# Scale and shift after a turn: one pass from PSUM on ScalarE and VectorE in place of two passes on VectorE and GpSimd

## The chip, the cores and the metric

The kernel runs on one core of a Trainium2 chip. The metric is the device time of one execution in microseconds (us), lower is better; it is given as the median of several executions. The engines are called by the profile's names: PE (TensorE matmul), PEld (TensorE weight load), DVE (VectorE), ACT (ScalarE), POOL (GpSimd) and SP (SyncE, here the queue that issues the transfers). A line number such as L352 is a line of the kernel before.

## The reference, cut to what matters

The model is a two-layer transformer over 512 latent tokens and 256 context tokens of width 1024. Each sub-layer is preceded by an RMS norm with a scale and a shift per channel; the feed-forward of layer 0 is followed by the norm that feeds layer 1's mixer, and that norm is what the change touches.

```python
def rms_norm(x, g):
    xf = x.astype(jnp.float32)
    y = xf * lax.rsqrt(jnp.mean(xf * xf, -1, keepdims=True) + NORM_EPS)
    return (y * g.astype(jnp.float32)).astype(x.dtype)

def modulate(h, shift, scale):
    return h * (1.0 + scale) + shift

for i in range(DEPTH):
    ...
    u = modulate(rms_norm(h, g_pre_mix[i]), sh_m, sc_m)
    uc = modulate(rms_norm(hc, g_pre_mix[i]), csh_m, csc_m)
    ...
    f = swiglu(modulate(rms_norm(h, g_pre_ffn[i]), sh_f, sc_f), w_ffn_gate[i], w_ffn_up[i], w_ffn_down[i])
    h = h + gt_f * rms_norm(f, g_post_ffn[i])
    ...
```

## The kernel before

Products are made of three float32r matmuls each: every operand is split into a high part (`hi`, a rounding copy on ACT, L181) and a low part (`lo`, a subtraction on DVE or POOL, L182), and the three cross products hi·hi, hi·lo and lo·hi are added up in PSUM. So ACT and DVE do a pass over every weight and every activation before PE can use it.

The tokens lie in six tiles of 128: tiles 0 to 3 are the latent tokens, 4 and 5 the context. The down product of layer 0's feed-forward (`dn`, L1696 to L1698) is made in three passes: the first 512 channels for all six tiles, then the second 512 channels for tiles 0 to 3, then the second 512 channels for tiles 4 and 5. In each pass a loop over 22 blocks of the hidden dimension loads weights (`raw_wd`), splits them (`hi_wd`, `lo_wd`), splits the block of hidden values (`gh` on ACT, `gl` on POOL in layer 0), and issues three matmuls for each tile.

When a tile of the second or third pass is complete, its rows are normed, gated and added to the residual `h` (`hbuf`, L1732 to L1739), and the generator `post_ffn0` hands it to `norm_T` (L341). `norm_T` takes the sum of squares (L337), the power -0.5 on POOL (L221, L228), scales the rows into `hn` (L345), and then, for each half of 512 channels, lets PE turn four blocks of 128x128 into one PSUM bank (`ptp`, L350), multiplies by the channel's scale from PSUM into `nt` (L352, DVE), adds the channel's shift in place (L353, POOL), and splits `nt` into `u1h` and `u1l`, the input of layer 1 (L181, L182). After the turn a channel is a partition, so scale and shift are one column (`a_col`, `s_col`) for each block of 128. `nt` has two buffers, `ptp` two banks. For latent tiles each half is split in two instructions of 128x256, because the tokens are also reordered; for context tiles in one of 128x512.

So the norm of tiles 0 to 3 runs while PE does the third pass of the down product (tiles 4 and 5), and the norm of tiles 4 and 5 while PE does the first product of layer 1 (`gq`, L523 to L525), which needs all four latent tiles. After it come four products for the neighbourhood attention's queries (`naqk`), then `gkv` and `nav`, which need the context tiles too. Beside them the modulation vectors of later norms are summed on DVE (`macc`, L254) from weights that SP fetches (`mraw`); their buffers lie in memory that the down product has used before.

The order of instructions on each engine is not the order of the program: the launch builds the kernel with a planner that keeps a simulated timeline and sorts the instructions of each engine by priority and by the times it expects. Each engine then runs its own list in order, so an instruction that waits holds everything behind it on that engine. SP issues its transfers in order too.

```python
with tile.TileContext(nc, schedule_with_timeline_sim=True) as tc:
    emit(tc, A)
...
ffn(0, U0, True, 6, close_u0, opened0, mods0, lambda: GGs['f0'], open_u1, post_ffn0)
...
tok_proj(A['wgq'], 512, range(4), lambda t, ps: head_norm(gqt[:, t, :], ps, 8, gqn, t, 1.0), uh, ul, "gq")
```

Of the kernel before, what the change touches and what calls it, by code (L numbers as in the profile page):

```python
# [154 lines left out]
AF = mybir.ActivationFunctionType  # L155
ALU = mybir.AluOpType
# [7 lines left out]
def emit(tc, A):  # L164
    nc = tc.nc
    V, S, G, T = nc.vector, nc.scalar, nc.gpsimd, nc.tensor
# [8 lines left out]
    def bc(ap, n):  # L175

        return ap.unsqueeze(len(ap.shape)).to_broadcast(list(ap.shape) + [n])

    def split(hi, lo, src, lo_eng=None):

        S.activation(hi, src, AF.Copy)  # L181
        (lo_eng or V).tensor_tensor(lo, src, hi.bitcast(F32), ALU.subtract)  # L182
# [151 lines left out]
    def rstd_of(src, junk):  # L334
        ss = sm.tile([128, 1], F32, tag="ss", name="ss")
        r = sm.tile([128, 1], F32, tag="rr", name="rr")
        S.activation(junk, src, AF.Square, scale=1.0 / 32.0, accum_out=ss)  # L337
        rsqrt_(r, ss, EPS)
        return r

    def norm_T(src, a_col, s_col, pst, hi_out, lo_out):  # L341

        hn = tmpp.tile([128, 1024], F32, tag="hn", name="hn", bufs=2)
        r = rstd_of(src, hn)
        S.activation(hn, src, AF.Copy, scale=r)  # L345
        yield
        for hf in range(2):
            ps = pst()
            for k in range(4):
                T.transpose(ps[:, k * 128:(k + 1) * 128], hn[:, (hf * 4 + k) * 128:(hf * 4 + k + 1) * 128], ident)  # L350
            t = tmpp.tile([128, 4, 128], F32, tag="nt", name="nt", bufs=2)
            V.tensor_tensor(t, ps.rearrange("p (k t) -> p k t", k=4), bc(a_col[:, hf * 4:hf * 4 + 4], 128), ALU.mult)  # L352
            G.tensor_tensor(t, t, bc(s_col[:, hf * 4:hf * 4 + 4], 128), ALU.add)  # L353
            for (h, l, sv) in zip(hi_out(hf), lo_out(hf), split_view(t, len(hi_out(hf)))):
                split(h, l, sv)

    class Lagged:

# [31 lines left out]
    def split_view(t, n):  # L390
        if n == 1:
            return [t]
        v = t.rearrange("p k (r b c) -> p k r b c", r=2, b=8)
        return [v[:, :, i] for i in range(2)]
# [36 lines left out]
    def ptp(name="ptp"):  # L431
        return bank("v", name)
# [181 lines left out]
    for d in range(2):  # L614
        rhs = gv[:, :, d * 8:(d + 1) * 8]
        ps = ptp("cum")
# [5 lines left out]
        ps = ptp("rest")  # L622
# [7 lines left out]
    for p in range(2):  # L630
        ps = ptp("tot")
# [1205 lines left out]
    def post_ffn0(t):  # L1837
        v = 0 if t < 4 else 1
        yield from norm_T(h[:, t, :], acol[v][:, 2, :], scol[v][:, 2, :], ptp, u_views(u1['h'], t), u_views(u1['l'], t))
# [470 lines left out]
```

## Time and profile before

| what | value |
|---|---|
| median of 3 runs | 1999.85 us (1995.31 to 2003.21) |
| the profiled execution | 1996.12 us |
| its span, first to last instruction | 1994.0 us |
| PE busy | 1830.4 us (92%) |
| DVE busy | 1436.1 us (72%) |
| ACT busy | 966.6 us (48%) |
| POOL busy | 928.0 us (47%) |
| mean granted TensorE clock | 0.956 |

The span is what the profile's rows cover; the execution's time is 2.1 us more. Busy shares are means over the whole span; the stretch that the change touches lies between 1229 and 1300 us and is read by itself below. A granted clock of 1.00 is TensorE's full level (2.4 GHz), 0.50 the half level (1.2 GHz).

### The profile page before, as it was taken

The numbers are of one execution on the slowest core, as the hardware profiler recorded it, in microseconds if no ns is written. First come the engines' busy times: TensorE is split into PE (matmuls) and PEld (weight loads), VectorE is DVE, ScalarE is ACT, GpSimd is POOL, SyncE is SP. The second block draws the span as 40 slices with busy tenths as digits, with TensorE's granted clock in tenths as the row PEclk, the third lists the DMA queues.
The fourth block names the chain that finished last, engine by engine and source line by source line (L and its number), as shares of the span: only waits on it lengthen the run. The fifth ranks groups of instructions, "written<-read, shape, count | busy, mean of one in ns | idle before, by whom it ended". The sixth has DMA issues, their size and how long they took to land.

```text
span 1994.0 us, 33781 instructions
## 1 busy us (share of the span) xinstructions
PE 1830.4 (92%) x12760; PEld 1504.2 (75%) x12760; DVE 1436.1 (72%) x2040; ACT 966.6 (48%) x1816; POOL 928.0 (47%) x828
## 2 busy tenths in 40 slices
PE   6989978989898979999999998889989959999998
PEld 3877855656566869999997776677655659999886
DVE  3686757677876696666656886887566589999654
ACT  4433457666874553333333345533455445445443
POOL 2387454344533376556547665653256142333101
PEclk7999978888999989999999999999999979999999
DMA  8255694665724613222227543586634212333221
GB/s 305 84 153 149 203 296 129 182 188 155 243 80 141 244 64 106 80 75 75 64 75 258 161 153 101 172 280 207 184 106 121 85 64 85 106 107 96 85 95 64
DMA packets 125751, 280.20 MB, mean 141 GB/s; under 512 B 12882, under 2 KB 43498, under 8 KB 125588
## 3 DMA queue, kind: packets, MB, share of 16 engines
q1 hardware_dynamic: 125588, 278.03, 44.0%
q8 instruction: 101, 1.65, 0.3%
q14 instruction: 62, 0.51, 0.1%
HBM read 226.15 MB, written 46.07 MB: 137 GB/s over the span
## 4 chain that ended last, share of the span: by engine, by line
PE 53%; DVE 9%; issue 4%; DMA 4%; POOL 3%; ACT 3%; SPq 0%; POOLq 0%; DVEq 0%; ACTq 0%
PE st L198 9%; PE st L199 9%; PE st L197 9%; PE dn L1696 4%; PE dn L1697 4%; PE dn L1698 4%; PE po L188 2%; DVE macc L254 2%; DMA mraw<-in_wmb_dram 2%; PE y L1410 1%; PE y L1411 1%; PE y L1412 1%; PE st L1958 1%; DVE ub L182 1%; PE st L1959 1%
## 5 line engine op out<-in xcount | busy, mean ns | idle before, releaser
L197 PE MATMUL st<-ub,hi_gu 128*128 128x384 f32 (+1 forms) x1232 | 385.8, 313 | 22.1 <-ACT ub L181 22.1
L198 PE MATMUL st<-ub,hi_gu 128*128 128x384 f32 (+1 forms) x1232 | 385.6, 313 | 1.1 <-DVE ub L182 1.0
L199 PE MATMUL st<-ub,lo_gu 128*128 128x384 f32 (+1 forms) x1232 | 384.3, 312 | 0.9 <-POOL lo_gu L182 0.9
L197 PEld LDWEIGHTS st<-ub,hi_gu 128*128 128x128 f32 x1232 | 233.9, 190 | 23.0 <-ACT ub L181 23.0
L199 PEld LDWEIGHTS st<-ub,lo_gu 128*128 128x128 f32 x1232 | 234.6, 190 | 1.6 <-POOL lo_gu L182 1.2
L198 PEld LDWEIGHTS st<-ub,hi_gu 128*128 128x128 f32 x1232 | 233.5, 190 | 2.0 <-DVE ub L182 2.0
L181 ACT ACTIVATE hi_gu<-s 128x512 fp32r<-128x512 f32 x176 | 111.1, 631 | 175.1 <-PE st L198 164.4
L1696 PE MATMUL dn<-hi_wd,gh 128*128 128x512 f32 x440 | 175.2, 398 | 2.2 <-ACT gh L181 2.2
L1697 PE MATMUL dn<-lo_wd,gh 128*128 128x512 f32 x440 | 175.0, 398 | 1.8 <-DVE lo_wd L182 1.8
L1698 PE MATMUL dn<-hi_wd,gl 128*128 128x512 f32 x440 | 165.3, 402 | 5.2 <-POOL gl L182 5.2
L182 DVE TENSOR_TENSOR lo_gu<-raw_gu,hi_gu 128x512 fp32r<-128x512 f32 x132 | 129.9, 998 | 42.8 <-ACT hi_gu L181 42.8
L182 DVE TENSOR_TENSOR lo_gu<-s,hi_gu 128x512 fp32r<-128x512 f32 x154 | 128.2, 833 | 45.1 <-ACT hi_gu L181 45.1
L254 DVE SCALAR_TENSOR_TENSOR macc<-mraw,cs,macc 128x1024 f32<-128x1024 f32 x80 | 125.5, 1592 | 22.8 <-DMA mraw<-in_wmb_dram 16.3
L181 ACT ACTIVATE hi_gu<-raw_gu 128x512 fp32r<-128x512 f32 x132 | 82.0, 629 | 98.8 <-PE st L198 91.9
L182 DVE TENSOR_TENSOR lo_wd<-raw_wd,hi_wd 128x512 fp32r<-128x512 f32 x110 | 96.8, 885 | 44.4 <-ACT hi_wd L181 44.3
L1606 POOL TENSOR_TENSOR s<-raw_gu 128x512 f32<-128x512 f32 x44 | 74.4, 1692 | 84.3 <-issue 70.7
L904 ACT ACTIVATE P<-st 128x512 f32<-128x512 f32 x128 | 73.0, 596 | 65.5 <-PE st L199 28.5
L1698 PEld LDWEIGHTS dn<-hi_wd,gl 128*128 128x128 f32 x440 | 82.3, 189 | 28.6 <-POOL gl L182 7.9
L1696 PEld LDWEIGHTS dn<-hi_wd,gh 128*128 128x128 f32 x440 | 83.0, 189 | 24.3 <-ACT gh L181 3.1
L181 ACT ACTIVATE gh<-g 128x512 fp32r<-128x512 f32 x76 | 47.5, 631 | 110.9 <-PE dn L1697 101.8
L1697 PEld LDWEIGHTS dn<-lo_wd,gh 128*128 128x128 f32 x440 | 83.0, 189 | 23.4 <-DVE lo_wd L182 2.7
L1662 POOL TENSOR_TENSOR g<-g,up 128x512 f32<-128x512 f32 x38 | 55.7, 1465 | 86.5 <-DVE up L1611 55.8
(545 smaller groups left out, 4794.7 us busy)
## 6 DMA issues: line engine op xcount, KB each, us to landing
mraw<-in_wmb_dram SPq DMA_DIRECT2D x56, 512.0 KB
raw_wd<-in_wd_dram SPq DMA_DIRECT2D x55, 512.0 KB
raw_gu<-in_wg_dram SPq DMA_DIRECT2D x44, 512.0 KB
raw_gu<-in_wu_dram SPq DMA_DIRECT2D x44, 512.0 KB
cu<-in_wmb_dram SPq DMA_DIRECT2D x24, 512.0 KB
raw_m<-in_wmb_dram SPq DMA_DIRECT2D x16, 512.0 KB
raw_qkv<-in_wqkv_dram SPq DMA_DIRECT2D x12, 512.0 KB
raw_tok<-qk_d SPq DMA_DIRECT2D x12, 512.0 KB
```

The lines of the kernel that those rows point to most:

```text
L181: S.activation(hi, src, AF.Copy)
L182: (lo_eng or V).tensor_tensor(lo, src, hi.bitcast(F32), ALU.subtract)
L197: T.matmul(out, wh, xh, start=start, stop=False)
L198: T.matmul(out, wh, xl, start=False, stop=False)
L199: T.matmul(out, wl, xh, start=False, stop=stop)
L254: V.scalar_tensor_tensor(a, raw, cs[:, self.k, v:v + 1], a, ALU.mult, ALU.add)
L904: S.activation(P[:, :n], ps[:, :n], AF.Exp)
L1606: G.tensor_tensor(s3, a11, a21, ALU.subtract)
L1662: G.tensor_tensor(g, g, u, ALU.mult)
L1696: T.matmul(ps, gh[:, tsl], wh, start=start, stop=False)
L1697: T.matmul(ps, gh[:, tsl], wl, start=False, stop=False)
L1698: T.matmul(ps, gl_[:, tsl], wh, start=False, stop=stop)
```

## The change

For each half of each tile the one multiply (DVE, 128x512) and the one add (POOL, 128x512) are replaced by four instructions of 128x128 that multiply and add in one pass from PSUM, with scale and shift as one value per partition: on ACT for the first half, on DVE for the second. Six tiles have two halves each, so 12 instructions of DVE and 12 of POOL go, and 24 of ACT and 24 of DVE come.

```diff
             t = tmpp.tile([128, 4, 128], F32, tag="nt", name="nt", bufs=2)
-            V.tensor_tensor(t, ps.rearrange("p (k t) -> p k t", k=4), bc(a_col[:, hf * 4:hf * 4 + 4], 128), ALU.mult)
-            G.tensor_tensor(t, t, bc(s_col[:, hf * 4:hf * 4 + 4], 128), ALU.add)
+            scaled(t, ps, a_col, s_col, hf)
             for (h, l, sv) in zip(hi_out(hf), lo_out(hf), split_view(t, len(hi_out(hf)))):
                 split(h, l, sv)
+
+    def scaled(x, ps, a_col, s_col, hf):
+
+        for k in range(4):
+            a, b = [c[:, hf * 4 + k:hf * 4 + k + 1] for c in (a_col, s_col)]
+            if hf == 0:
+                S.activation(x[:, k, :], ps[:, k * 128:(k + 1) * 128], AF.Identity, scale=a, bias=b)
+            else:
+                V.tensor_scalar(x[:, k, :], ps[:, k * 128:(k + 1) * 128], a, b, ALU.mult, ALU.add)
```

## Rows read from the trace of the kernel before

**Rows 1.** By stretch: length, busy PE, PEld, DVE, ACT, POOL (counts), PEclk, DMA share, GB/s

```profile
1236.25:1272.40 36.15, 28.82 (x133) 21.63 (x131) 36.15 (x46) 26.10 (x57) 31.72 (x35) 1.00 0.38 119
1272.40:1300.00 27.60, 26.94 (x127) 22.45 (x128) 21.69 (x31) 15.59 (x26) 12.29 (x16) 1.00 0.67 209
1320.00:1340.00 20.00, 15.26 (x103) 14.85 (x103) 17.30 (x23) 3.36 (x7) 10.43 (x11) 0.83 0.88 294
```

**Rows 2.** Groups by line and shape, 1236.2 to 1272.4 us: busy, mean ns | idle before

```profile
L182 DVE TENSOR_TENSOR u1l<-nt,u1h 128x256 fp32r<-128x256 f32 x13 | 11.0, 881 | 0.0
L1698 PE MATMUL dn<-hi_wd,gl 128*128 128x512 f32 x32 | 10.9, 420 | 5.2 <-POOL gl L182 5.2
L353 POOL TENSOR_TENSOR nt<-nt,scol 128x512 f32<-128x512 f32 x8 | 10.5, 1307 | 3.9 <-DVE nt L352 3.5 <-PE dn L1698 0.5
L352 DVE TENSOR_TENSOR nt<-ptp,acol 128x512 f32<-128x512 f32 x8 | 5.3, 677 | 0.0
L181 ACT ACTIVATE u1h<-nt 128x256 fp32r<-128x256 f32 x14 | 5.0, 405 | 4.5 <-POOL nt L353 4.5
```

**Rows 3.** Timeline of PE: start, length, instruction [idle before, releaser]

```profile
1249.17 0.73 PE L1698 MATMUL dn<-hi_wd,gl 128*128 128x512 f32 x2 [0.89 <-POOL gl L182]
1260.90 0.73 PE L1698 MATMUL dn<-hi_wd,gl 128*128 128x512 f32 x2 [1.76 <-POOL gl L182]
1269.61 0.50 PE L523 MATMUL gq<-hi_gq,u1h 128*128 128x512 f32 x1 [1.50 <-ACT u1h L181]
1273.06 1.21 PE L525 MATMUL gq<-hi_gq,u1l 128*128 128x512 f32 x4 [1.34 <-DVE u1l L182]
```

**Rows 4.** Timeline of POOL: start, length, instruction

```profile
1240.21 1.23 POOL L353 TENSOR_TENSOR nt<-nt,scol 128x512 f32<-128x512 f32 x1
1241.40 1.18 POOL L182 TENSOR_TENSOR gl<-gm,gh 128x256 fp32r<-128x256 f32 x1
1246.83 0.83 POOL L221 TENSOR_SCALAR rr<-ssd 128x1 f32<-128x1 f32 x1
```

**Rows 5.** Groups by line and shape of ACT, whole span

```profile
L181 ACT ACTIVATE wo_h<-raw_o 128x1024 fp32r<-128x1024 f32 x8 | 8.3, 1055 | 6.8 <-DMA raw_o<-in_wo_dram 6.8
L345 ACT ACTIVATE hn<-hbuf,rr 128x1024 f32<-128x1024 f32 x6 | 6.9, 1148 | 4.2 <-POOL rr L228 4.2
L1664 ACT ACT_TABLE_LOAD x2 | 2.6, 1283 | 0.0
L1885 ACT ACTIVATE gkt<-gkv 128x128 f32<-128x128 f32 x6 | 1.8, 306 | 0.0
```

**Rows 6.** Timeline of ACT: start, length, instruction [idle before, releaser]

```profile
1241.64 0.71 ACT L181 ACTIVATE u1h<-nt 128x256 fp32r<-128x256 f32 x2
1278.30 1.15 ACT L345 ACTIVATE hn<-hbuf,rr 128x1024 f32<-128x1024 f32 x1 [0.61 <-POOL rr L228]
```

**Rows 7.** Groups by line and shape of DVE, whole span

```profile
L1609 DVE TENSOR_TENSOR p<-p,st 128x384 f32<-128x384 f32 x22 | 12.2, 553 | 18.4 <-PE st L199 18.4
L1609 DVE TENSOR_TENSOR p<-p,st 128x256 f32<-128x256 f32 x22 | 9.0, 409 | 0.4 <-PE st L199 0.2
L182 DVE TENSOR_TENSOR lo_wk<-raw_wk,hi_wk 128x128 fp32r<-128x128 f32 x4 | 1.3, 320 | 2.3 <-ACT hi_wk L181 2.3
```

**Rows 8.** Timeline of the DMA queue of SP

```profile
1279.48 0.33 SPq L1444 DMA_DIRECT2D hbuf<-in_gpost_dram  x1
1279.90 0.86 SPq L252 DMA_DIRECT2D mraw<-in_wmb_dram  x2
```

**Rows 9.** Timeline of PE, later

```profile
1322.12 0.38 PE L523 MATMUL gkv<-hi_gkv,u1h 128*128 128x256 f32 x1 [1.79 <-DVE xl L1923]
1329.77 0.58 PE L523 MATMUL gkv<-hi_gkv,u1h 128*128 128x256 f32 x1 [2.96 <-DVE xl L1923]
```

**Rows 10.** Busy time by stretch, the four us around the later waits

```profile
1326.00:1330.00 4.00, 1.04 (x8) 0.84 (x8) 3.11 (x3) 0.27 (x1) 3.70 (x4) 0.87 0.85 295
1330.00:1334.00 4.00, 4.00 (x20) 4.00 (x21) 3.04 (x4) 1.61 (x4) 1.21 (x2) 0.50 0.88 257
```

## Prediction, made blind

> **What bounds the kernel now.** The busy shares of the page make PE the bound over the whole span, but the change touches one stretch only, so I read that stretch by itself, in this order: the busy time by stretch, the groups of instructions inside it, the timelines of PE and POOL there, and then what SP and PE do behind it.
>
> In the stretch from the first turned tile to the last `u1h` of tile 3, 36.15 us, no engine has much room: DVE is busy all the time, POOL 31.7 us, PE 28.8 us, ACT 26.1 us [rows 1]. The reader should see that PE is not the bound here. Its matmuls wait 5.2 us in all, in six waits, all of them for `gl`, the low part that POOL makes [rows 2]. The timeline of POOL shows why: an add of the norm (L353, 1.23 us at 1240.21) stands in front of the `gl` that PE wants [rows 4], and in the order of POOL's list the same holds for five of the six waits, the longest (1.76 us) among them. The other one (0.89 us, at 1249.17) ends a `gl` behind the small powers of the norm, L221 and L228 [rows 3, 4]. After the down product PE waits twice more, 1.50 us for the first `u1h` and 1.34 us for the `u1l` of tile 3 [rows 3]: that is the latency of the norm itself. Together PE idles 5.2 + 1.5 + 1.34 = 8.0 us between 1236 and 1274 us. That is the pot, 0.4% of the execution.
>
> DVE is full partly because its subtractions are slow there: `u1l` of 128x256 takes 881 ns [rows 2], while a DVE instruction of the same shape with an input in PSUM takes 409 ns [rows 7].
>
> **The change, part by part.** *POOL loses 12 adds.* Eight lie in the stretch, 10.5 us at a mean of 1307 ns [rows 2]; POOL goes from 31.7 to about 21 us busy. The five waits behind an add are 5.2 - 0.9 = 4.3 us, and these I count as gained. The 0.9 us behind the powers stays.
>
> *DVE loses 12 multiplies and gets 24 narrow ones.* A multiply costs 677 ns [rows 2], all twelve 8.1 us. No row shows a DVE pass from PSUM of 128x128 with two column operands. From 128x384 to 128x256 the time falls from 553 to 409 ns, 144 ns for 128 columns [rows 7], so 128x128 would be about 265 ns; the high end is the 320 ns of a 128x128 subtraction with both inputs in SBUF [rows 7], the low end the 144 ns of its columns alone. 24 x 0.265 = 6.4 us (3.5 to 7.7), so DVE gains about 1.7 us over the six tiles (0.4 to 4.6), some 1.1 us of it in the four latent ones. With a third of POOL's work gone (10.5 of 31.7), I take a third of the delay off DVE's subtractions: 13 x (881 - 409) ns = 6.1 us on `u1l`, a third is 2 us. DVE is then no longer full at 36 us; about 33 us are left to do.
>
> *ACT gets 24 passes.* No row has an ACT pass with two column operands either. A copy of 128x128 from PSUM takes 306 ns [rows 5]. One column operand as scale costs 1148 - 1055 = 93 ns, the difference of two copies of the same size [rows 5]. The bias I bound between nothing and another 93 ns: 399 to 492 ns. Two passes in a row take 0.71 us where one takes 405 ns [rows 2, 6], so neighbours overlap by 0.10 us and a pass costs the queue 0.30 to 0.39 us. I take 0.38, since a second column should cost what the first does. The stretch gets 16 of them, 16 x 0.38 = 6.1 us (4.8 to 6.3), all six tiles 9.1 us (7.2 to 9.4). What hides them is ACT's idle time, 36.15 - 26.10 = 10.05 us [rows 1], if the stretch stays as long; queued behind them are the splits `gh` and `hi_wd`, for which PE would wait.
>
> The Trainium skill (ScalarE: Activation LUTs, What ACT_TABLE_LOAD costs) speaks against the first half on ScalarE in particular: it states 186 ns plus 0.833 ns a column, 93 ns for each column operand, and an overlap of 93 ns between neighbours. By that a pass is an estimated 479 ns, 386 ns in the queue, and 16 of them 6.2 us; that differs little from the 6.1 us above, and the trace's 93 ns for one operand agrees [rows 5].
>
> *The latency of a half* falls. Before, it is a DVE pass of 677 ns, a wait, a POOL pass of 1307 ns and then the split [rows 2]; after, four passes of ACT, about 1.6 us, with no other engine between them and the split `u1h` on ACT. The 1.50 us for `u1h` should go, the 1.34 us for `u1l` most likely too.
>
> **The sum.** At best PE gets 4.3 + 1.5 + 1.3 = 7.1 us. But ACT would then have 26.1 + 6.1 = 32.2 us of work in 36.15 - 7.1 = 29.05 us. If nothing of it can move, ACT sets the stretch at 32.2 us and the gain is 3.95 us. Some of it can move: the splits of the next product's weights sit in the stretch, and ACT is busy only 15.6 of the 27.6 us behind it [rows 1]. Between 4 and 7.1 us I take 5.
>
> Does the gain last? Behind the stretch the DMA queues are nearly full (share 0.88 from 1320 to 1340 us [rows 1]), so a later start of transfers could eat it. The transfer that opens this run, `hbuf` at 1279.48, goes out when `hn` of tile 4 is finished, 1278.30 + 1.15 [rows 6, 8], and SP holds the `mraw` loads behind it [rows 8]. Tile 4 comes out of the down product, so when PE ends that product 4 to 5 us earlier, the whole run of transfers moves with it. The change issues no transfer of its own. Tiles 4 and 5 are normed under `gq`, while PE is busy 26.9 of 27.6 us [rows 1]; their eight ACT and eight DVE passes cost nothing there, and 3 us of ACT if the cover were gone.
>
> The profiled execution took 1996.1 us, so the sum gives 1991. The median of the three runs lies 3.7 us higher, 1999.85; against it the same 5 us give 1995, my forecast.
>
> **The rivals.** *The gain is used up behind the stretch* (chance 0.22). The planner puts in order again everything from the changed tiles on, with its own durations; the sums of `macc` on DVE and the full DMA queues could take back 5 us. Time: 2000. For it: 0.88 DMA share. Against it: the run of transfers starts from tile 4, which comes earlier.
>
> *The next gap closes too* (0.18). At 1322 and 1329.8 us PE waits 1.79 and 2.96 us for DVE [rows 9], and after the second wait the granted clock is 0.50; in the eight us shown the missing clock is 4 x (0.13 + 0.50) = 2.5 us [rows 10]. A DVE list in another order could avoid both: 5 + 4.75 + 2.5 = 12 us, 1988. Nothing in the profile says that it will; the waits hang on `mraw` loads too.
>
> *ACT becomes the bound* (0.1, the other side). If the planner puts each block of four passes in front of the `gh` that PE wants next, all 24 are exposed: 24 x 0.38 = 9.1 us, and with one gap long enough for the half clock, 2.5 us more: +11.6 us, 2011. It decides from the point where ACT's work in the stretch exceeds the 36.15 us, that is with 10 us added; 6.1 are expected. For it: ACT is in order and PE reads `gh` within a few us. Against it: POOL's wait is the last to end today, not ACT's.
>
> *Another order makes one more gap* of the kind at 1322 to 1330 us, with no gain left: 4.75 + 2.5 = 7 us, 2007 (0.07).
>
> *The ACT function costs a table load.* The kernel before has no Identity; a load takes 1283 ns [rows 5], and two for each of six tiles would be 15 us. The Trainium skill (ScalarE: Activation LUTs, Table sets: the hidden batching unit) says that identity, like copy, is in every set; then there is none. I give it 0.02, at 2015.
>
> The forecast itself has what is left, 0.41, with 1991 to 1999 as its own range.
>
> **How the numbers follow.** This kernel can be told from no change at about 0.5%, 10 us. Faster by more than that needs the second rival, or the forecast with luck in the order: 0.18. Slower by more needs ACT as the bound, the table load, or half of the extra gap: 0.14. The rest, 0.68, is within 10 us. The range 1984 to 2008 reaches over the second rival to the extra gap and leaves out 0.17.
>
> **What would show it.** Right: no POOL add on nt; 24 ACT passes of 0.4 to 0.5 us and 24 DVE passes of about 0.27 us; PE's waits for `gl` down from 5.2 to about 1 us; the first `gq` matmul 4 to 6 us earlier than 1269.6; `hbuf` on SP equally earlier; `u1l` under 881 ns. Wrong: PE waiting for `gh` or `hi_wd` from ACT in the stretch, a table load there, or a `gq` that starts earlier while the end of the span does not move: then the order behind it, and not this edit's costs, made the time.

## The result, and the profile after

The changed kernel takes 1986.32 us (median of 4 executions, 1983.3 to 1988.37) beside 2001.53 us for the kernel before (4 executions); the ratio (changed over before, below 1 is faster) is 0.9945, with an interval of 0.9922 to 0.9969. The two medians alone lie further apart, 15.2 us or 0.9924, near the lower end of that interval. Two later comparisons of the same two kernels gave 0.9953 and 0.9966 (below). Of 2000 us these ratios are 11, 9.4 and 6.8 us. The forecast was 5 us and 1995.

The profiled execution after took 1986.34 us, its span is 1984.6 us; before these were 1996.12 and 1994.0 us. The page's busy times of the changed kernel:

```profile
PE 1828.9 (92%) x12760; PEld 1505.4 (76%) x12760; DVE 1429.4 (72%) x2052; ACT 972.6 (49%) x1840; POOL 917.0 (46%) x816
```

Here the change can be counted: DVE 24 - 12 = 12 instructions more, ACT 24 more, POOL 12 fewer. Nothing of this size says where the time went; the stretch does. Its groups by line and shape, 1230.1 to 1264.7 us, after (busy, mean ns | idle before; lines from 357 on are eight higher than before, so L1706 is L1698 of before):

```profile
L182 DVE TENSOR_TENSOR lo_wd<-raw_wd,hi_wd 128x512 fp32r<-128x512 f32 x14 | 11.0, 811 | 0.3 <-ACT hi_wd L181 0.3
L1706 PE MATMUL dn<-hi_wd,gl 128*128 128x512 f32 x32 | 10.6, 413 | 1.8 <-POOL gl L182 1.8
L182 DVE TENSOR_TENSOR u1l<-nt,u1h 128x256 fp32r<-128x256 f32 x16 | 6.9, 473 | 0.4 <-ACT u1h L181 0.4
L361 ACT ACTIVATE nt<-ptp,scol,acol 128x128 f32<-128x128 f32 x16 | 6.0, 460 | 0.0
L363 DVE TENSOR_SCALAR nt<-ptp,acol,scol 128x128 f32<-128x128 f32 x16 | 5.4, 400 | 0.1
```

Beside [rows 2]: PE's wait for `gl` is 1.8 us where it was 5.2; `u1l` takes 473 ns where it took 881; the two new passes take 460 ns on ACT and 400 ns on DVE. The weights' subtraction `lo_wd`, 811 ns after, is quicker too; in the kernel before, 1236.2 to 1272.4 us:

```profile
L182 DVE TENSOR_TENSOR lo_wd<-raw_wd,hi_wd 128x512 fp32r<-128x512 f32 x14 | 13.2, 954 | 0.0
```

These waits are left in PE's timeline of the changed kernel:

```profile
1241.57 0.73 PE L1706 MATMUL dn<-hi_wd,gl 128*128 128x512 f32 x2 [0.92 <-POOL gl L182]
1243.55 0.73 PE L1706 MATMUL dn<-hi_wd,gl 128*128 128x512 f32 x2 [0.23 <-POOL gl L182]
1249.53 0.73 PE L1706 MATMUL dn<-hi_wd,gl 128*128 128x512 f32 x2 [0.65 <-POOL gl L182]
1260.72 0.50 PE L531 MATMUL gq<-hi_gq,u1h 128*128 128x512 f32 x1 [2.28 <-ACT u1h L181]
...
1312.39 0.39 PE L531 MATMUL gkv<-hi_gkv,u1h 128*128 128x256 f32 x1 [1.01 <-DVE xl L1931]
1318.23 0.39 PE L531 MATMUL gkv<-hi_gkv,u1h 128*128 128x256 f32 x1 [2.83 <-DVE xl L1931]
```

Against [rows 3] three short waits for `gl` stand in place of six, and the wait for `u1l` (1.34) is gone. In POOL's list each of the three ends a `gl` directly behind a power (L228). But the wait for `u1h` has grown from 1.50 to 2.28 us. ACT's timeline of the changed kernel shows what it was doing ahead of that `u1h`:

```profile
1255.58 1.51 ACT L361 ACTIVATE nt<-ptp,scol,acol 128x128 f32<-128x128 f32 x4
1256.95 1.18 ACT L181 ACTIVATE hi_gq<-raw_gq 128x512 fp32r<-128x512 f32 x2
1258.24 0.60 ACT L1733 ACTIVATE junk<-dn 128x512 f32<-128x512 f32 x1
...
1258.83 0.71 ACT L181 ACTIVATE u1h<-nt 128x256 fp32r<-128x256 f32 x2
1259.44 0.62 ACT L181 ACTIVATE hi_gq<-raw_gq 128x512 fp32r<-128x512 f32 x1
1259.96 0.71 ACT L181 ACTIVATE u1h<-nt 128x256 fp32r<-128x256 f32 x2
```

The four passes of tile 3's first half end at 1257.09, but two `hi_gq` splits and a sum of squares stand before its `u1h` in ACT's list, and one more split before the `u1h` of the second half, which ends at 1260.67; PE starts at 1260.72. ACT idles 0.1 us there in all. By stretch, after, with the columns of [rows 1] (first turned tile to the first `gq`, on to the first `gkv`, on to the last `nav`):

```profile
1230.10:1260.70 30.60, 26.50 (x125) 19.93 (x123) 29.87 (x56) 30.36 (x74) 22.97 (x28) 1.00 0.44 137
1260.70:1309.70 49.00, 48.90 (x212) 39.36 (x213) 40.81 (x57) 23.18 (x44) 20.06 (x21) 0.97 0.77 247
1309.70:1366.10 56.40, 52.56 (x297) 45.97 (x296) 42.92 (x51) 15.94 (x38) 30.89 (x28) 0.97 0.75 244
```

In the first row ACT is busy 30.36 and DVE 29.87 of 30.60 us: POOL has become free and two other engines are full. The third stretch in the kernel before, same view:

```profile
1318.60:1377.50 58.90, 53.82 (x297) 47.18 (x296) 46.31 (x55) 16.24 (x38) 33.55 (x31) 0.94 0.74 242
```

It was 2.5 us longer, with as many matmuls (297). In this pair of profiles that is the granted clock, 0.94 before and 0.97 after (58.9 x 0.06 = 3.5 us against 56.4 x 0.03 = 1.7), and the two waits for `xl`, 1.79 and 2.96 us before [rows 9], 1.01 and 2.83 after. But other profiles of the same kernels show something else. In two more of the kernel before (e1 and e11, below) the stretch is longer still, and its clock is 0.97 as well; the waits for `xl` add up to 4.4 to 4.8 us in three profiles before and to 3.8 to 4.7 in three after. What e1 and e11 have and no profile of the changed kernel does is a wait at a `nav` matmul, in e1:

```profile
1343.94 0.50 PE L523 MATMUL nav<-hi_nav,u1h 128*128 128x512 f32 x1 [3.17 <-ACT gvt L1886]
```

In e11 it is 3.38 us, in the first profile 0.34. ACT owes that `gvt`, and in e1 it stands behind another instruction in ACT's list, a sum of squares of `gq` (`hsq`) that waits for POOL:

```profile
1343.09 0.63 ACT L1874 ACTIVATE hsq<-gqt 128x512 f32<-128x512 f32 x1 [4.22 <-POOL gqt L387]
1343.63 0.26 ACT L1886 ACTIVATE gvt<-gkv 128x128 f32<-128x128 f32 x1
```

In ACT's list of the changed kernel this `hsq` stands three weight splits ahead of the first copies of `gkv`, and the wait is not there.

**A warning about two single profiles.** The two spans differ by 9.4 us, but the changed execution was already 6.2 us ahead at its first turned tile (1230.1 against 1236.3), before the norm comes into play, and each engine's list up to there is the same in both programs. So I compare stretches by their distance from the first turned matmul (L350), over three profiles of each kernel: before, e1 and e11 are the old one, after, e2 and e10 the new one. The columns are the start of the first matmul of `gq`, the first of `gkv`, the last of `nav`, and the end of the span, in us, each rounded for itself.

| kernel | first turn at | to `gq` | to `gkv` | to last `nav` | `gkv` to `nav` | to the end |
|---|---|---|---|---|---|---|
| before | 1236.3 | 33.3 | 82.4 | 141.2 | 58.9 | 757.7 |
| e1_same | 1233.3 | 33.4 | 83.1 | 143.2 | 60.2 | 762.8 |
| e11_same | 1241.7 | 33.4 | 83.6 | 144.0 | 60.5 | 764.0 |
| after | 1230.1 | 30.6 | 79.7 | 136.0 | 56.4 | 754.5 |
| e2_again | 1232.4 | 30.7 | 79.6 | 136.3 | 56.8 | 755.1 |
| e10_again | 1233.2 | 30.7 | 79.6 | 136.7 | 57.2 | 755.6 |

By the means the gain is 2.7 us up to `gq`, 0.7 us from `gq` to `gkv`, 3.1 us from `gkv` to the last `nav`, 6.5 us together, and 6.4 us at the end (761.5 against 755.1): what is won by the last `nav` is kept. The start of the first turn scatters over 8.4 us in the unchanged kernel alone, so I don't count the 6.2 us of lead. That it is chance is not shown: all three changed profiles have their first turn earlier than all three of the kernel before, by 5.2 us in the means, and more profiles would have to say whether a part of it belongs to the program.

### The profile page after: what moved, and what is told of

Read it like the earlier page. It is cut to its first block, busy times and chain, and to the rows that moved or that the text cites. A ratio compares the mean times of both kernels' runs of the same rounds, so it can differ in the third digit from the quotient of the medians.

```text
span 1984.6 us, 33787 instructions
## 1 busy us (share of the span) xinstructions
PE 1828.9 (92%) x12760; PEld 1505.4 (76%) x12760; DVE 1429.4 (72%) x2052; ACT 972.6 (49%) x1840; POOL 917.0 (46%) x816
## 4 chain that ended last, share of the span: by engine, by line
PE 63%; DVE 8%; ACT 5%; issue 3%; DMA 3%; POOL 2%; SPq 0%; POOLq 0%; ACTq 0%; DVEq 0%
PE st L197 10%; PE st L198 10%; PE st L199 10%; PE dn L1704 4%; PE dn L1705 4%; PE dn L1706 4%; PE po L188 3%; DVE macc L254 2%; PE y L1418 1%; PE y L1419 1%; PE y L1420 1%; PE st L1966 1%; PE st L1967 1%; PE rm L269 1%; PE naqk L197 1%
## 5 line engine op out<-in xcount | busy, mean ns | idle before, releaser
L1706 PE MATMUL dn<-hi_wd,gl 128*128 128x512 f32 x440 | 165.5, 403 | 1.8 <-POOL gl L182 1.8
L182 DVE TENSOR_TENSOR lo_gu<-raw_gu,hi_gu 128x512 fp32r<-128x512 f32 x132 | 130.2, 999 | 43.2 <-ACT hi_gu L181 43.1
L1706 PEld LDWEIGHTS dn<-hi_wd,gl 128*128 128x128 f32 x440 | 82.7, 190 | 25.3 <-POOL gl L182 4.4
```

The source lines that it names most:

```text
L1706: T.matmul(ps, gl_[:, tsl], wh, start=False, stop=stop)
```

## The experiments

The theory on trial is that of the prediction: POOL's adds stood before `gl`, their going is the gain, and it is kept as far as the engine that takes the work has room. Its rivals: the gain is DVE's own (narrow passes in place of wide ones), or it comes from the order that the planner makes behind the norm, or from chance. The expectations call the theory A and the rival of each run B or C. Every edit also lets the planner sort the lists anew, so an experiment rarely changes one thing alone.

**The kernels repeated.** e1_same is the kernel before, e2_again the changed kernel.

> The kernel before, unchanged: it says how far two builds of one program lie apart. My theory: about 6 of the 9.4 us between the two profiled spans arose ahead of the change's first instruction, where the order is the same, and are chance between executions; so the ratio here is 1.000 within 0.003, and the first turned tile of this profile (1236.3 us in the one shown) may lie anywhere between 1229 and 1238 us. Rival: the lead ahead of the change belongs to the changed program; then this profile has its first turned tile at 1236 us again, within 1.5 us.

> The changed kernel once more. My theory: only what happens from the first turned tile on is the change's, 3 to 6 us, ratio 0.997 to 0.9985; the first turned tile lies between 1229 and 1238 us as it falls out. Rival (the lead is the program's): ratio 0.9945 again, first turned tile at 1230 us again within 1.5 us.

Measured: e1_same 0.9984 (0.9971 to 0.9997), e2_again 0.9953 (0.9936 to 0.9970). The unchanged kernel can come out 0.16% beside itself, so a ratio's last 0.2% says little; the changed kernel lies outside that. Its ratio is below the 0.997 that I expected of the change alone, and its first turn, at 1232.4 us, is not where the rival had it: neither reading came out whole.

**One half at a time.** e3_act_half changes the first half only (ACT), e4_dve_half the second only (DVE):

```diff
-            scaled(t, ps, a_col, s_col, hf)
+            if hf == 0:            # e4: hf == 1
+                scaled(t, ps, a_col, s_col, hf)
+            else:
+                V.tensor_tensor(t, ps.rearrange("p (k t) -> p k t", k=4), bc(a_col[...], 128), ALU.mult)
+                G.tensor_tensor(t, t, bc(s_col[...], 128), ALU.add)
```

> Only the first half of each tile is changed (four passes of ACT from PSUM); the second half keeps the multiply on DVE and the add on POOL. My theory (POOL's adds stand in front of gl): half of the adds go, so PE's waits for gl fall from 5.2 to about 3 us, and the wait for u1h before the first gq matmul goes as in the full change; the norm's stretch gains 2 to 3.5 us, ratio 0.998 to 0.999. Rival (the narrow passes on DVE and its fewer, faster subtractions make the gain): no gain here, ratio 1.000.

> Only the second half of each tile is changed (four passes of DVE from PSUM); the first half keeps DVE and POOL. My theory: half of the adds go, waits for gl fall to about 3 us, but the first half's way through DVE and POOL stays, and with it the 1.5 us wait for u1h: gain 1.5 to 3 us, ratio 0.9985 to 0.9995. Rival (DVE's relief makes the gain): most of the full change's gain is here, 4 us or more after the first turned tile.

Measured: e3 0.9996 (0.9984 to 1.0008), e4 0.9962 (0.9946 to 0.9978); `gq` comes 35.0 and 32.7 us after the first turn. Both expectations missed: e3, which should have gained 2 to 3.5 us, gained nothing, as its rival had it, and e4's ratio can't be told from the full change's. So e3 is slower in the norm than the kernel before (33.4), and its waits are still POOL's: one line of PE's timeline of e3, then three of POOL's.

```profile
1248.07 1.22 PE L1710 MATMUL dn<-hi_wd,gl 128*128 128x512 f32 x2 [2.83 <-POOL gl L182]
```

```profile
1244.95 1.42 POOL L356 TENSOR_TENSOR nt<-nt,scol 128x512 f32<-128x512 f32 x1 [0.78 <-DVE nt L355]
1246.33 0.99 POOL L228 TENSOR_TENSOR rr<-rr,nhalf 128x1 f32<-128x1 f32 x1
1247.30 4.14 POOL L182 TENSOR_TENSOR gl<-gm,gh 128x256 fp32r<-128x256 f32 x4
```

The add that is left waits for DVE's multiply, and the `gl` that PE wants waits behind it. Halving the adds did not halve the waits: they are 5.6 us in all (5.2 before). In e4 the wait for `gl` is down to 0.4 us, and others are there; the waits of PE in its norm stretch (total, times, longest):

```profile
PE gq L535 <- ACT u1h L181: 3.4, 1, 3.4
PE dn L1709 <- DVE lo_wd L182: 1.2, 3, 0.5
PE dn L1710 <- POOL gl L182: 0.4, 1, 0.4
```

Up to `gq` e4 gains 0.7 us only, with DVE busy for all of the 32.7 us; the rest of its gain, to 3 us at the end of its one profile, lies behind `gkv` and was not taken apart.

**POOL's load put back.** e5_pool_back is the changed kernel with twelve more POOL adds of the old shape, whose sum nothing reads:

```diff
             scaled(t, ps, a_col, s_col, hf)
+            d = tmpp.tile([128, 4, 128], F32, tag="ntd", name="ntd", bufs=1)
+            G.tensor_tensor(d, t, bc(s_col[:, hf * 4:hf * 4 + 4], 128), ALU.add)
```

> The changed kernel with POOL's twelve adds put back beside it: each half's add of the shift is made once more by POOL into a tile that nobody reads. Theory A (POOL's adds stood in front of gl, and slowed DVE's subtractions): the stretch from the first turned tile to the first gq matmul goes from 30.6 back to 32.5 us or more, the waits for gl from 1.8 to 4 us or more, and u1l from 473 to over 700 ns; ratio 0.997 to 0.999. Rival B (the gain is the chain without an engine change, or the order that the planner finds, not POOL's time): stretch at 30.6 within 0.7 us, ratio 0.994 to 0.996.

Measured: 1.0017 (1.0002 to 1.0032), `gq` at 35.6. Groups of e5, 1232.2 to 1268.4 us:

```profile
L354 POOL TENSOR_TENSOR ntd<-nt,scol 128x512 f32<-128x512 f32 x8 | 14.3, 1789 | 2.0 <-DVE nt L365 1.9
L1708 PE MATMUL dn<-hi_wd,gl 128*128 128x512 f32 x32 | 10.9, 422 | 5.1 <-POOL gl L182 5.1
L182 DVE TENSOR_TENSOR u1l<-nt,u1h 128x256 fp32r<-128x256 f32 x13 | 8.7, 710 | 0.0
```

The wait for `gl` is back at 5.1 us (5.2 before), and `u1l` is at 710 ns. All of the gain is gone, though ACT and DVE do the new passes. More was put back than had been taken away: the eight adds take 14.3 us here and took 10.5 [rows 2]. The planner's order changed too, so the sizes are not POOL's alone; but the new passes alone are not the gain.

**POOL freed, DVE loaded.** e6_add_dve is the kernel before with the add on DVE; e7_all_dve is the changed kernel with both halves on DVE:

```diff
-            G.tensor_tensor(t, t, bc(s_col[...], 128), ALU.add)     # e6
+            V.tensor_tensor(t, t, bc(s_col[...], 128), ALU.add)
-            if hf == 0:                                            # e7
+            if hf < 0:
```

> The kernel before with one letter changed: the add of the shift stays a pass of its own of 128x512, but on DVE. POOL has no adds, ACT gets nothing, DVE gets 12 passes of 0.6 to 1.2 us. Theory A (POOL's time): waits for gl fall to 2 us or less, but DVE, which is full, becomes later by 8 x 0.6 = 5 us less what it waits less for POOL: stretch 31 to 33.5 us, ratio 0.996 to 0.999. Rival B (one pass from PSUM makes the gain): stretch 33.3 us or more, ratio 1.000 or more.

> Both halves as four passes of DVE from PSUM, none on ACT. Each block of four took 1.36 us on DVE in the changed kernel. Theory A: POOL as in the full change, gl waits below 2 us, DVE as full as before (8 x 1.3 = 10.4 us in place of 4.8 for the multiplies, less 6 us that its subtractions wait less): stretch 30.5 to 32.5 us, and the first u1h no longer behind ACT's own queue; ratio 0.994 to 0.997. Rival B (the half on ACT carries the gain): stretch 33 us, ratio 0.999 or more.

Measured: e6 1.0010 (0.9993 to 1.0027), e7 0.9989 (0.9970 to 1.0007). By stretch, first turn to `gq`, first e6, then e7:

```profile
1235.50:1272.50 37.00, 26.55 (x125) 19.85 (x123) 37.00 (x57) 25.65 (x58) 23.38 (x28) 0.97 0.45 135
```

```profile
1229.90:1264.30 34.40, 27.15 (x126) 20.05 (x124) 34.40 (x67) 25.88 (x57) 23.02 (x28) 1.00 0.47 137
```

DVE is busy 37.00 of 37.00 and 34.40 of 34.40 us, POOL has a third free in both. The wait for `gl` is gone, and PE's largest waits in that stretch are, first in e6, then in e7:

```profile
PE gq L523 <- ACT u1h L181: 6.8, 1, 6.8
PE dn L1697 <- DVE lo_wd L182: 1.9, 2, 1.2
```

```profile
PE gq L531 <- ACT u1h L181: 4.6, 1, 4.6
PE dn L1705 <- DVE lo_wd L182: 2.5, 6, 0.8
```

ACT, which owes that `u1h`, stands idle for DVE's `nt`; in ACT's timeline of e6 the last one:

```profile
1271.76 0.72 ACT L181 ACTIVATE u1h<-nt 128x256 fp32r<-128x256 f32 x2 [4.41 <-DVE nt L353]
```

Both came out as rival B had it, e7 at the edge. So an empty POOL is not worth anything by itself (e6, e7), nor is one pass from PSUM (e7); and the half on ACT isn't either while POOL's adds stay (e3, e5). The gain in the norm needs both: POOL's adds gone, and the work in ACT's 10 us of idle time [rows 1] rather than on DVE.

**Which half goes where.** e8_swap puts the first half on DVE and the second on ACT; e9_last_swap does that for tile 3 alone, to have the last `u1h` follow its own passes on ACT:

```diff
-            if hf == 0:
+            if hf == 1:                  # e8
+            if (hf == 0) != flip:        # e9: flip is t == 3
```

> First half on DVE, second on ACT. Same load on each engine as in the changed kernel. If loads make the gain (theory A): stretch 30 to 31.5 us and ratio 0.994 to 0.997, as the change. If the order that the planner finds makes it (rival C): a stretch off by more than 1.5 us either way.

> The changed kernel, but for tile 3, the last that the first gq matmul waits for, the first half is on DVE and the second on ACT. In the changed kernel PE waits 2.3 us there for a u1h that stands behind two weight splits and a sum of squares in ACT's list. If that list is what the wait hangs on: the wait falls below 1 us, the stretch from the first turned tile to the first gq matmul from 30.6 to 29 to 30 us, ratio to before 0.993 to 0.996. If the planner only puts the wait elsewhere: 30.6 us or more.

Measured: e8 0.9970 (0.9953 to 0.9987), `gq` at 31.4, so which half goes to which engine makes no difference in the time that can be told, though `gq` comes 0.7 us later; e9 0.9948 (0.9932 to 0.9964), 1986.4 us beside 1990.61 for the changed kernel in the same comparison, `gq` at 30.8. In e9 the wait for `u1h` is gone, as expected, but `gq` did not come earlier than in the changed kernel (30.6 to 30.7). One line each of PE and POOL in e9, and DVE beside them:

```profile
1265.81 0.74 PE L1706 MATMUL dn<-hi_wd,gl 128*128 128x512 f32 x2 [2.23 <-POOL gl L182]
```

```profile
1260.88 4.88 POOL L182 TENSOR_TENSOR gl<-sg,gh 128x256 fp32r<-128x256 f32 x1 [0.70 <-ACT gh L181]
```

```profile
1260.73 0.68 DVE L182 TENSOR_TENSOR lo_wd<-raw_wd,hi_wd 128x512 fp32r<-128x512 f32 x1
1261.33 0.75 DVE L182 TENSOR_TENSOR u1l<-nt,u1h 128x256 fp32r<-128x256 f32 x2
1262.00 1.89 DVE L182 TENSOR_TENSOR lo_gq<-raw_gq,hi_gq 128x512 fp32r<-128x512 f32 x3
1263.81 0.76 DVE L182 TENSOR_TENSOR u1l<-nt,u1h 128x256 fp32r<-128x256 f32 x2
1264.48 0.68 DVE L182 TENSOR_TENSOR lo_gq<-raw_gq,hi_gq 128x512 fp32r<-128x512 f32 x1
```

One subtraction of POOL (128x256; one of the same shape takes 1.18 us in [rows 4]) takes 4.88 us; DVE runs nine subtractions with two inputs in SBUF without a gap from 1260.73 to 1265.16, and POOL ends 0.60 us behind them. That is the largest of the new waits for `gl`, 4.0 us in all. What e9 has over the changed kernel comes later, from `gkv` to `nav` (51.8 us against 56.4 to 57.2), and was not taken apart; its interval overlaps the changed kernel's. So another order of the same work can be worth as much behind the norm as the change itself.

**The changed kernel and the one before again**, beside e9:

> The changed kernel a third time, to size it. From the first turned tile on the changed kernel was 5.4 us shorter than the kernel before (two profiles of each). If that is all, the ratio is 0.997 within 0.0015; if something ahead of the change belongs to it, 0.9945 within 0.0015, and the first turned tile lies at 1232 us or earlier again.

> The kernel before once more, beside the run above on the same chip: ratio 1.000 within 0.002, stretch from the first turned tile to the first gq matmul 33.3 us within 0.3 us, first turned tile between 1229 and 1238 us.

Measured: e10_again 0.9966 (0.9952 to 0.9980), e11_same 0.9991 (0.9972 to 1.0010). Their stretches stand in the table; e11's first turn, 1241.7 us, lies outside the 1229 to 1238 that I expected.

**Only the context tiles' adds put back.** The gain behind `gq` could be the order that the planner makes or the four adds of tiles 4 and 5. e12_pool_ctx is the changed kernel with e5's useless add for tiles 4 and 5 alone:

```diff
             scaled(t, ps, a_col, s_col, hf)
+            if again:                # t >= 4
+                d = tmpp.tile([128, 4, 128], F32, tag="ntd", name="ntd", bufs=1)
+                G.tensor_tensor(d, t, bc(s_col[...], 128), ALU.add)
```

> The changed kernel with POOL's adds put back (into a tile that nobody reads) for the two context tiles only, whose norm runs behind the stretch. From the first gkv matmul to the last nav the kernel before took 58.9 to 60.5 us and the changed one 56.4 to 57.2. If POOL's adds for the context tiles make that second gain: the norm's stretch stays at 30.6 us within 0.7, gkv to nav goes to 58.5 us or more, ratio to before 0.9975 to 0.999. If it comes from the order that the planner found or from an earlier start: gkv to nav stays at 56 to 57.5 us, ratio 0.995 to 0.9975.

Measured: 0.9976 (0.9962 to 0.9989). The lists of DVE, ACT and POOL are those of the changed kernel over the whole span but for the four adds, so here the order is not in play; `gq` comes at 30.7 us, `gkv` at 79.5. Then `gkv` to `nav` takes 59.7 us, as in the kernel before (58.9 to 60.5). Two adds in POOL's timeline of e12, and two sums in DVE's:

```profile
1280.64 1.04 POOL L355 TENSOR_TENSOR ntd<-nt,scol 128x512 f32<-128x512 f32 x1 [5.44 <-ACT nt L364]
1284.18 1.35 POOL L355 TENSOR_TENSOR ntd<-nt,scol 128x512 f32<-128x512 f32 x1 [2.50 <-DVE nt L366]
```

```profile
1280.65 2.11 DVE L254 SCALAR_TENSOR_TENSOR macc<-mraw,cs,macc 128x1024 f32<-128x1024 f32 x1
...
1284.56 2.06 DVE L254 SCALAR_TENSOR_TENSOR macc<-mraw,cs,macc 128x1024 f32<-128x1024 f32 x1
```

The same two instructions in DVE's timeline of the changed kernel:

```profile
1280.27 1.29 DVE L254 SCALAR_TENSOR_TENSOR macc<-mraw,cs,macc 128x1024 f32<-128x1024 f32 x1
...
1283.35 1.28 DVE L254 SCALAR_TENSOR_TENSOR macc<-mraw,cs,macc 128x1024 f32<-128x1024 f32 x1
```

Each takes 0.8 us more beside a POOL add, DVE falls back by 1.6 us, without idle time between the two sums, and PE sees it at `gkv`, in e12's timeline and stretch:

```profile
1314.59 0.39 PE L534 MATMUL gkv<-hi_gkv,u1h 128*128 128x256 f32 x1 [3.06 <-DVE xl L1934]
1320.43 0.58 PE L534 MATMUL gkv<-hi_gkv,u1h 128*128 128x256 f32 x1 [2.81 <-DVE xl L1934]
```

```profile
1309.80:1369.50 59.70, 53.82 (x297) 47.24 (x296) 43.10 (x53) 15.96 (x38) 33.48 (x29) 0.94 0.73 235
```

The first wait is 3.06 us where it was 1.01, and the granted clock 0.94 where it was 0.97. The Trainium skill (SBUF — State Buffer, Who interferes with whom) says that VectorE and GpSimd share one pair of SBUF ports and that it is taken exclusively; the 1.29 and 2.11 us here, and the 4.88 us of e9, agree.

So POOL's adds for the context tiles cost 2.4 to 3.2 us of this stretch in the changed kernel's order. By its ratio e12 can't be told from the changed kernel, as the intervals overlap. At the end of its profile it is 5.8 us behind, and half of that arises behind `nav` and was not taken apart. And it is not shown that the kernel before loses its 3.1 us this way: e12 loses them at `xl`, where the kernel before waits only 0.3 us more than the changed one in the mean of three profiles, and has no wait at `nav`, where two of the three profiles of the kernel before lose over 3 us.

## Why the prediction was right, and where its sizes were off

The forecast's mechanism held in the norm: POOL's adds stood before `gl` (e5), and it took ACT's idle time to gain by their going (e6, e7). The time, 1986.32 us, lies in the wide range, but not in the 1991 to 1999 that the forecast gave as its own; it is nearer to the 1988 of the rival *the next gap closes too*. A part of that may be luck of the executions: the gain is 6.4 us by the table and 6.8 to 11 us by the ratios, and the medians lie 15.2 us apart. That 6.4 is near 5 is in part luck too, as the 5 us are made up otherwise than the sum had it.

*The waits for `gl`*: 4.3 us were to go, 3.4 went (5.2 to 1.8). I left 0.9 us standing at the powers; the three waits that are left, 1.8 us, all end a `gl` behind one. The longest wait of the kernel before (1.76 us) had a power of 0.75 us between the add and the `gl`, so I was wrong to count it as the add's alone.

*The latency of a half*: the 1.34 us for `u1l` went, as forecast. The 1.50 us for `u1h` "should go" and became 2.28. This step failed. I costed the passes and the split behind them, 1.6 us, and not ACT's list between them: two `hi_gq` splits and a sum of squares. Of the best case of 7.1 us the stretch kept 2.7, not 5. e9 shows that moving that wait does not help either: the next one, of 2.23 us, is there at once. The cap that the sum put on it, ACT's own work, was of the right kind: ACT is busy 30.36 of 30.60 us.

*ACT's pass*: 458 ns in the mean of 24, 399 to 492 forecast, and a block of four 1.51 us, 0.35 each in the queue (0.38 taken). No table load came: seven groups with nine loads, as before. The rival of the table load is out, and so is ACT as the bound for all 24 passes; nothing shows PE waiting for `gh` or `hi_wd` in the norm. POOL does wait for ACT's `gh` now, 2.7 us in six waits.

*DVE's pass* was the mis-sized term: 401 ns, where 265 was taken and 320 was the high end. A block of four takes 1.37 us, so 24 passes cost 24 x 0.32 = 7.7 us of queue, the multiplies 8.1 by their durations; DVE won 0.4 us there at most, not 1.7. The extrapolation came from instructions without column operands. What made up for it is *the relief of DVE's subtractions*: 13 x (881 - 473) ns = 5.3 us where a third of 6.1, 2 us, was taken, and 14 x (954 - 811) ns = 2 us on `lo_wd` that the sum did not have. The relief is not in proportion to the adds that go: `u1l` takes 456 and 446 ns already in e3 and e4, with half of them left, and 549 and 513 ns in e6 and e7, with none. The errors are of opposite sign; the relief is the larger.

*Does the gain last?* Yes, and it grows. `hbuf` goes out at 1266.01, 35.9 us after the first turn, before 43.2; that is 7.3 us earlier, not 4 to 6. But e12 has its first `hbuf` at the same distance (36.0) and no second gain, so the earlier transfers don't make it by themselves. "Tiles 4 and 5 ... cost nothing there" looked at PE under `gq` only: in e12 their POOL adds delay DVE, whose lateness PE pays some 30 us later at `gkv`. The rival *the next gap closes too* did not come as it was put: the two gaps at `xl` are hardly shorter (4.5 us before, 4.3 after in the means). Most of the 3.1 us, 2.3 in the means, is the wait for `gvt` at `nav` that went with the new order of ACT's list, and this wait the prediction did not have: the profile that it was read from shows 0.34 us there, and loses its time by the lower clock. e12, which has the new order and the adds, doesn't have the wait. So the second gain looks in good part like the planner's order; no run tests that order alone, and how much is POOL's adds stays open. The rival *the gain is used up* is out.

From `gq` to `gkv` little was won (0.7 us, though the 1.34 us for `u1l` fell there): after the wait of 2.28 us the granted clock of that stretch, a mean over the levels 1.00 and 0.50, is 0.97 in all three profiles of the changed kernel and 1.00 in all three of the kernel before; 49 x 0.03 = 1.5 us.

Open: how much of the difference between 6.4 us and the ratios' 6.8 to 11 us is chance, how the second gain divides between POOL's adds and the order, and what e4 and e9 won behind `gkv`.

## What to carry to other kernels

Moving work off a slow engine pays only as far as the engine that takes it has idle time in that stretch: the same edit with the work on the full engine gave nothing (e6, e7). Ask what stands in the taker's list between the moved instruction and the one that is waited for, and what the old engine was slowing down beside it, also where the stretch itself seems covered. With a gain below a per cent, compare stretches from a common event over several profiles; the ends of two single ones of the same kernel differ by more than the effect. One pair of profiles can also show other losses than the next: the wait for `gvt` is 0.34 us in the first profile of the kernel before and over 3 us in the two others.

## What was not expected of the hardware

A DVE pass of 128x128 from PSUM with two column operands takes 401 ns, nearly as long as the 409 ns of a 128x256 addition with an input in PSUM [rows 7]. POOL's work slows DVE beside it: `u1l` of 128x256 takes 473 ns after and 881 before, and a sum of 128x1024 goes from 1.29 to 2.11 us beside one POOL add of 1.04 us. And the other way round a row of nine DVE subtractions goes with a POOL subtraction of 4.88 us (e9), where one of the same shape takes 1.18 us in [rows 4].
